# A hybrid decoder step: cached latents turned as raw float32 rows and split behind the turn, pacing constant 7.1 to 6.7

## Chip, cores and metric

The kernel runs on one core of a Trainium2 chip. The metric is the device time of one execution in microseconds (us); the number compared is the median of several executions. PE is the matrix engine, DVE the vector engine, ACT the scalar engine, POOL the GpSimd engine, SP the engine that issues most transfers.

## The reference, cut to what matters

One step of a one-layer decoder over 1024 prompt tokens and 8 sample batches of 8 tokens. One input projection yields all branches; the change lies in the attention of the sample batches over their cached past:

```
ckv_past = cache_ckv[page_table]            # (8 batches, 2048 keys, 256 features)
kpe_past = cache_kpe[page_table]            # (8, 2048, 32)
q_abs  = einsum('bthd,rhd->bthr', q_nope, w_uk)
s_past = einsum('bthr,bpr->bhtp', q_abs, ckv_past) + einsum('bthd,bpd->bhtp', q_pe, kpe_past)
...
p = softmax(concat([s_past, s_new]) * ATTN_SCALE)
o_lat = einsum('bhtp,bpr->bthr', p_past, ckv_past) + einsum('bhts,bsr->bthr', p_new, c_kv)
```

Beside it, and independent of it, stands the big product h @ W_in for all 1088 tokens.

## The kernel before, in words

Products with float32 accuracy are made of float32r passes: a number is split into `hi` (rounded to float32r, on ACT or POOL) and `lo` (the rest, on DVE), and `mm3` (lines 76 to 81) issues three passes hi·hi, hi·lo, lo·hi. Where accuracy asks for no product, as in a transpose (`tp`, line 67), one pass is enough.

The attention of the sample goes through blocks: 8 batches, each with four blocks of 512 cached keys (j = 0 to 3; 32 such blocks in all) and one small block of its own new tokens (j = 4). A block of 512 keys goes through these steps.

- `fetch` (line 623): POOL issues an indirect gather of 512 KB into `raw` (two buffers). POOL rounds it to the hi half of `nat`, DVE takes the lo half (lines 645, 646); `nat` too has two buffers. Rotary keys go through `skn` in the same way.
- `turn_keys` (line 651): PE turns rows into columns: two transposes of the rotary keys (`ptk`) and sixteen of the latents (`ptt`, four for each of hi and lo and of two feature halves), each 128 by 128. Four of them fill a PSUM bank, and each bank is copied out to a tile `tt`, hi banks by ACT and lo banks by DVE (line 669).
- `attend` (line 673): scores (`pss`: four passes of 512 columns, one for each `tt`, and two short ones), maximum and exponential on ACT and DVE (`stmp`, `spr`), transposes of the probabilities (`ptp`), their split (`spt`), and the weighted sum of the latents in their natural layout (`spo`: eight passes over `nat`). After the fifth block of a batch the parts are put together (`sacc`) and turned (`pto`).

Between these steps PE is given dense work: `dense` yields the remaining input projection in triples of passes of 362 or 364 columns (`pj`). How much stands between two steps is decided by a counter, `clk`, that adds an estimate for each pass issued (`cost`, line 60: 4.18e-4 us for each column, whatever the kind of pass). `sample_attention` (line 742) turns the next block when the counter is `PACE` beyond the end of the turn before. The order is then laid out, engine by engine, by a list scheduler that may move a row a little; each engine runs its rows strictly in that order. When the sample's attention is done, what is left of the dense work follows without gaps, then the q latents, the latents of the prompt, its attention, and the output.

Of the kernel before, what the change touches and what calls it, by code (L numbers as in the profile page):

```python
# [9 lines left out]
F32 = mybir.dt.float32  # L10
# [8 lines left out]
P = 128  # L19
D = 1024  # L20
NP = 1024            # prompt tokens
NB, NT = 8, 8        # sample batches, tokens each
# [9 lines left out]
NU = 3 + NP + NB * 11            # convolution input with its histories  # L32
# [3 lines left out]
# columns of the per-feature vectors  # L36
V_BSH, V_BSC, V_NW, V_QW, V_CW, V_CB, V_BA, V_BX, V_LAM, V_H0, V_ST = 0, 8, 16, 24, 26, 42, 46, 50, 54, 58, 90
V_ALL = V_ST + 4 * 24
# columns of the shape constants
# [4 lines left out]
def trunk_step(ctx: ExitStack, tc: tile.TileContext, a, o):  # L44
# [3 lines left out]
    PACE = 7.1  # L48
# [4 lines left out]
    def split(hi, lo, src):  # L53
        """src = hi + lo, each of them in float32r"""
        S.copy(hi, src)  # L55
        V.tensor_tensor(lo, src, f(hi), OP.subtract)  # L56

    clk = [0.0]                 # about how many us of products have been issued
# [12 lines left out]
    def mm4(out, lhs, rhs, start, stop, beside=1):  # L71
        """plain float32 product; beside: how many run at once in other columns of the array"""
        clk[0] += 4 * cost(out) / beside
        T.matmul(out, lhs, rhs, start=start, stop=stop)

    def mm3(out, lhs, rhs, start, stop):
        """float32 product out of three float32r passes; lhs, rhs = (hi, lo)"""
        clk[0] += 3 * cost(out)
        T.matmul(out, lhs[0], rhs[0], start=start, stop=False)  # L79
        T.matmul(out, lhs[0], rhs[1], start=False, stop=False)  # L80
        T.matmul(out, lhs[1], rhs[0], start=False, stop=stop)  # L81
# [7 lines left out]
    g_dram = dram.tile([20, P, N], F32, name="g_dram")      # gA, mA, mB before their sigmoids  # L89

    # ------------------------------------------------------------- constants
    vec = const.tile([P, V_ALL], F32, name="vec")
    cst = const.tile([P, C_ALL], F32, name="cst")
    sgs = const.tile([P, D], F32, name="sgs")            # gate in partial sums; row 9: its bias
# [17 lines left out]
    ats = const.tile([P, 4, NS], F32, name="ats")        # attention of the sample, feature by token  # L112

    def rms_pow(out, ss, width, tmp):
        """out = (ss / width + eps) ** -0.5"""
        n = out.shape[0]
        G.tensor_scalar(tmp, ss, 1.0 / width, EPS, OP.mult, OP.add)  # L117
        G.tensor_tensor(out, tmp, nhalf[:n], OP.pow)

    # features of the recurrent branch: convolution input, then gated output  # L120
    # (the first two tiles hold weights before)
# [3 lines left out]
    # ================================================== everything that is projected from h  # L125
    with ExitStack() as px_:
# [3 lines left out]
        sc = hp.tile([P, KC, 32], F32, name="sc")        # silu(c)  # L130
        hs = hp.tile([P, KC, NS], F32, name="hs")        # h of the sample
# [5 lines left out]
        def weights(src, halves=(0, 1), w=None):  # L137
            """one tile of 128 columns: [p, k, 128] as hi, lo"""
# [16 lines left out]
        # -------------------------------------------- h, feature by feature  # L155
        with ExitStack() as pb, tc.manual_schedule(engines={mybir.EngineType.PE}):
# [4 lines left out]
            # silu(c)  # L161
            S.activation(sc, cT, AF.Sigmoid)
            V.tensor_tensor(sc, sc, cT, OP.mult)
            # softplus(-lambda), with log1p(e) = 2 atanh(e / (2 + e))
# [20 lines left out]
            # shift and scale of every feature: [feature, prompt | 8 batches]  # L185
# [8 lines left out]
            def ada_sum(aw):  # L194
                """rows 32 t + j: partial sums over k of c_j @ 256 columns"""
# [29 lines left out]
            def x_norm(i):  # L225
                """128 tokens over their rms"""
# [9 lines left out]
            def x_turn(i):  # L236
                """feature by token"""
# [8 lines left out]
            def h_part(k, s, n):  # L246
                """modulated features of some tokens; two tiles of the recurrent branch serve until that needs them"""
# [64 lines left out]
        # -------------------------------------------- the other projections  # L312
# [6 lines left out]
        def project(w, done, groups=GRP, beside=()):  # L319
            """128 columns of the input projection; beside: what is issued after each group of tokens"""  # L320
# [10 lines left out]
        def gate_sums(k, q):  # L331
            """partial sums of 128 columns of the modulation's gate: rows 32 t + j"""
# [21 lines left out]
        def gate_lru(c):  # L354
            """the recurrent branch times silu(gB)"""
            def done(g, s, n, ps):
                U = L[c]
                sg = cc.tile([P, 364], F32, name="ev", bufs=2)
                # silu(g) = g / 2 (1 + tanh(g / 2)); tanh has its place beside exp
# [17 lines left out]
        def dense():  # L377
            """the projections that no one waits for, to be put between the steps of what has to wait"""
# [17 lines left out]
        def fill(us):  # L396
            """dense work for about so many us"""
# [4 lines left out]
        with ExitStack() as pd:  # L402
# [11 lines left out]
            # rows of 16 keys (rotary keys) and of 4 keys (latents): (page * 8 + p % 8) * 4 + quarter  # L414
# [3 lines left out]
            cnew = cc.tile([NS, 512], F32R, name="cnew")      # new latents of the sample: hi | lo  # L418
            knew = cc.tile([NS, 64], F32R, name="knew")       # new rotary keys of the sample: hi | lo
            ctn = cc.tile([P, 2, 2, NS], F32R, name="ctn")    # new latents, feature by token: [r, hi | lo, half, token]  # L420
            ktn = cc.tile([P, NS], F32R, name="ktn")
            V.memset(f(ktn[64:128]), 0.0)
            qa = cc.tile([P, 2, H, NS], F32, name="qa")       # queries of the latents: [r, half, head, token]
            qr = cc.tile([P, H, NS], F32, name="qr")          # rotary queries, four times along the rows
            ol = cc.tile([P, 2, H, NS], F32, name="ol")       # attended latents
# [3 lines left out]
            def kv_finish(i, m, ps, tmp_pool, ck_pool):  # L429
                """latent and rotary key of up to 128 tokens, and their outputs"""  # L430
# [10 lines left out]
                for j in range(2):                      # the other half beside  # L441
# [8 lines left out]
            # ---------------------------------------- queries and new keys of the sample, token by token  # L450
            def sample_queries(kq):
                ps = bank("pkvq")               # [kv; q]
# [22 lines left out]
                # normed q latent  # L475
# [21 lines left out]
                # queries: [half of the heads and token, head, 64 | rotary | rotary swapped]  # L497
# [14 lines left out]
                # feature by [half of the heads, head, token]  # L512
# [9 lines left out]
                # through the keys' up projection  # L522
# [7 lines left out]
            # ---------------------------------------- convolution, gates and scan of the recurrent branch  # L530
            def recurrence(p2):
                for c in range(4):
# [37 lines left out]
                    # 1 - exp(2 log_a) = tanh(-log_a) (1 + a a)  # L570
# [4 lines left out]
                    # the position before each sample starts its recurrence: a = 0, b = h0  # L575
# [9 lines left out]
            def interleave(*streams):  # L585
                """streams yield how long their next step has to wait; meanwhile the others, else dense work"""
# [19 lines left out]
            # ---------------------------------------- attention of the sample  # L606
            with ExitStack() as pq:
# [15 lines left out]
                def fetch(b, j):  # L623
                    """page rows as hi and lo"""
                    if j == 0:
                        # [r, half, hi | lo of (head, token)], and the rotary part for even and odd keys
# [22 lines left out]
                    return nat, kn  # L649

                def turn_keys(b, j, got):
                    """keys by rows: feature by token"""
# [3 lines left out]
                    nat, kn = got  # L656
# [5 lines left out]
                    tt = [[None, None], [None, None]]  # L662
                    for i in range(2):
                        for r in range(2):
                            pt_ = bank("ptt", F32R, (P, 4, P))
                            for k in range(4):
                                tp(pt_[:, k, :], nat[:, i, KEY[k], P * r:P * r + P], ident_r)
                            t_ = p4.tile([P, 512], F32R, name="tt", bufs=6)
                            (S.copy if i == 0 else V.tensor_copy)(t_, f(pt_).rearrange("p a b -> p (a b)"))  # L669
                            tt[r][i] = t_  # L670
                    return tt, kt_

                def attend(b, j, got, turned):
                    """512 keys of the past, or the new ones (j = 4): their part of the attention, with its own maximum"""
# [4 lines left out]
                    # scores: products, then the sum of the hi and lo halves of the queries and the maximum  # L679
# [12 lines left out]
                    else:                       # the keys of other batches have no part  # L692
# [10 lines left out]
                    # probabilities by keys, and the latents that they weigh  # L703
# [8 lines left out]
                    for k in range(nt):  # L712
                        for i in range(2):
                            mv = got[0][:, i, KEY[k], :] if j < 4 else cnew[:, 256 * i:256 * i + 256]
# [8 lines left out]
                    # the parts together  # L723
# [18 lines left out]
                def sample_attention():  # L742
                    todo = [(b, j) for b in range(NB) for j in range(5)]
                    got = fetch(*todo[0])
                    live = []                   # [ready, stream]
# [36 lines left out]
            # values out of the latents, two heads at a time  # L782
# [24 lines left out]
        # -------------------------------------------- latents of the prompt, and the first keys and queries  # L807
# [5 lines left out]
        # keys of a head, feature by token: 64 latent rows, then the rotary key twice  # L813
# [42 lines left out]
        def latent_turn(i, acc):  # L856
            """latents of 128 tokens, feature by token"""
# [7 lines left out]
        def rotary_keys(g, acc):  # L865
            """rotary keys of half of the prompt, feature by token"""
# [6 lines left out]
        with ExitStack() as pq:  # L873
            # q latent without its 1 / rms: that goes into the rotary tables. Its squares stay where tables
            # and keys come later
# [28 lines left out]
            # rotary keys of the prompt, twice side by side  # L904
# [481 lines left out]
```

## Time and profile before

| what | value |
|---|---|
| median of 3 runs | 1009.61 us (1009.12 to 1012.59) |
| span of the profiled execution | 1014.5 us |
| PE busy | 979.5 us, 97% of the span |
| DVE, ACT, POOL busy | 653.5, 505.5, 235.8 us (64%, 50%, 23%) |
| sample attention, first to last transpose of latents | 197.8 to 554.5 us |

The profiled execution's own time is its span; no other part of it is shown. It lies 4.9 us over the median of the runs shown. A busy share counts a pipelined pass longer than the time by which it delays the next one, so prices of passes are best read from the distance between starts or from the chain of work that ended last, where pieces do not overlap.

### The profile page before, as it was taken

To read this page: it belongs to the slowest core of one execution; us is meant where nothing else is said; L and a number is where in the kernel's file an instruction comes from. 1 tells how busy PE (TensorE), PEld (TensorE's weight loads), DVE (VectorE), ACT (ScalarE), POOL (GpSimd) and SP (SyncE) were. 2 spreads that over 40 slices of the span, in tenths; PEclk is the share of its full clock that TensorE was granted. 3 is DMA by queue.
4 is the path that set the end of the run, shared out by engine and by line. 5 is a ranking of instruction groups with operands and counts; after the bars stand their busy time and mean duration, and the time that the engine had idled before them with its cause. 6 is when DMAs were issued, how large, how long until landed. Compare 5 with 4: busy or idle time off the path is not lost.

```text
span 1014.5 us, 17199 instructions
## 1 busy us (share of the span) xinstructions
PE 979.5 (97%) x6317; PEld 885.0 (87%) x6317; DVE 653.5 (64%) x1486; ACT 505.5 (50%) x1182; POOL 235.8 (23%) x312
## 2 busy tenths in 40 slices
PE   4899999999999999999999999999999999999997
PEld 3676999899999999999999889888888899998886
DVE  5773664556565767665565536888879976882643
ACT  6455655444444444444444433767768854651211
POOL 5442221321112111111110013534444400000101
PEclk9998999999999999999999999999999999999999
DMA  9852123444333332243222212100010155652331
GB/s 327 297 136 78 55 95 103 139 139 137 106 114 105 102 104 87 86 123 112 85 93 67 75 52 62 38 13 21 12 32 11 36 179 167 197 176 72 127 102 63
DMA packets 52102, 104.67 MB, mean 103 GB/s; under 512 B 8177, under 2 KB 23601, under 8 KB 50994
## 3 DMA queue, kind: packets, MB, share of 16 engines
q1 hardware_dynamic: 46626, 84.69, 25.9%
q0 software_dynamic: 5392, 18.88, 6.5%
q8 instruction: 50, 0.82, 0.3%
q14 instruction: 34, 0.28, 0.1%
HBM read 85.58 MB, written 16.92 MB: 101 GB/s over the span
## 4 chain that ended last, share of the span: by engine, by line
PE 72%; DVE 4%; ACT 3%; issue 1%; DMA 0%; POOL 0%; POOLq 0%; SPq 0%; DVEq 0%; ACTq 0%
PE pj L79 9%; PE pj L81 8%; PE pj L80 8%; PE ptt L69 4%; PE pss L65 4%; PE spo L65 3%; PE py L79 3%; PE py L80 3%; PE py L81 3%; PE pout L81 3%; PE pout L80 3%; PE pout L79 3%; PE ptr L1019 2%; PE po L1036 1%; PE ptp L69 1%; PE sc L79 1%
## 5 line engine op out<-in xcount | busy, mean ns | idle before, releaser
L79 PE MATMUL pj<-hh,whi 128*128 128x362 f32 (+2 forms) x656 | 228.4, 348 | 0.0
L80 PE MATMUL pj<-hl,whi 128*128 128x362 f32 (+2 forms) x656 | 219.0, 334 | 0.0
L81 PE MATMUL pj<-hh,wlo 128*128 128x362 f32 (+2 forms) x656 | 218.9, 334 | 0.0
L79 PEld LDWEIGHTS pj<-hh,whi 128*128 128x128 f32 x656 | 124.5, 190 | 10.4 <-issue 4.9
L80 PEld LDWEIGHTS pj<-hl,whi 128*128 128x128 f32 x656 | 124.8, 190 | 2.3 <-issue 0.9
L81 PEld LDWEIGHTS pj<-hh,wlo 128*128 128x128 f32 x656 | 124.6, 190 | 2.2 <-issue 0.9
L645 POOL TENSOR_SCALAR nat<-raw 128x1024 fp32r<-128x1024 f32 x32 | 34.5, 1078 | 192.4 <-PE spo L65 189.0
L1005 POOL TENSOR_SCALAR pr<-pr,mx 128x128 f32<-128x128 f32 (+3 forms) x64 | 49.4, 772 | 88.5 <-DVE mx L1004 80.1
L1002 ACT ACTIVATE pr<-sc,mx 128x128 f32<-128x128 f32 (+3 forms) x64 | 47.7, 746 | 13.5 <-DVE mx L1000 12.5
L1000 DVE TENSOR_REDUCE mx<-sc 128x1 f32<-128x128 f32 (+3 forms) x64 | 48.1, 751 | 7.6 <-PE sc L998 7.3
L69 PE MATMUL ptt<-ident_r,nat 128*128 128x128 f32 x512 | 49.8, 252 | 1.1 <-POOL nat L645 1.1
L56 DVE TENSOR_TENSOR spt<-ptp,spt 128x256 fp32r<-128x256 f32 (+1 forms) x40 | 15.2, 380 | 51.3 <-ACT spt L55 51.2
L69 PEld LDWEIGHTS ptt<-ident_r,nat 128*128 128x128 f32 x512 | 46.3, 142 | 1.4 <-POOL nat L645 1.4
L56 DVE TENSOR_TENSOR ptl<-ptr,pth 128x512 fp32r<-128x512 f32 (+1 forms) x80 | 45.4, 576 | 3.3 <-ACT pth L55 2.3
L1260 ACT ACTIVATE ot<-xo 128x512 f32<-128x512 f32 (+2 forms) x19 | 11.5, 606 | 72.2 <-DVE xo L1259 67.9
L1019 PE MATMUL ptr<-ident,pr 128*128 128x128 f32 x288 | 45.2, 275 | 1.5 <-DVE ptl L56 1.3
L689 ACT COPY stmp<-pss 64x512 f32<-64x512 f32 (+1 forms) x40 | 20.0, 500 | 52.7 <-PE pss L65 52.5
L117 POOL TENSOR_SCALAR ost<-ost 128x1 f32<-128x1 f32 (+1 forms) x9 | 2.9, 325 | 183.7 <-DVE ost L1263 183.7
L55 ACT CAST pth<-ptr 128x512 fp32r<-128x512 f32 (+1 forms) x80 | 40.0, 502 | 10.2 <-PE ptr L1019 9.2
L56 DVE TENSOR_TENSOR wlo<-wraw,whi 128x512 fp32r<-128x512 f32 x58 | 39.9, 703 | 6.5 <-ACT whi L55 6.3
L646 DVE TENSOR_TENSOR nat<-raw,nat 128x1024 fp32r<-128x1024 f32 x32 | 39.1, 1222 | 7.3 <-POOL nat L645 7.1
L669 DVE CAST tt<-ptt 128x512 fp32r<-128x512 f32 x64 | 41.1, 682 | 3.6 <-PE ptt L69 1.0
(469 smaller groups left out, 2629.5 us busy)
## 6 DMA issues: line engine op xcount, KB each, us to landing
wraw<-w_in SPq DMA_DIRECT2D x60, 256.0 KB, 3.3
sg<-g_dram SPq DMA_DIRECT2D x16, 544.0 KB, 3.8
aw<-ada_ss SPq DMA_DIRECT2D x8, 1024.0 KB, 7.6
g_dram<-ev SPq DMA_DIRECT2D x40, 181.0 KB, 3.0
wraw<-ada_g SPq DMA_DIRECT2D x16, 256.0 KB, 2.9
oraw<-w_out SPq DMA_DIRECT2D x16, 256.0 KB, 3.6
xo<-xp SPq DMA_DIRECT2D x8, 512.0 KB, 5.2
out_y<-xo SPq DMA_DIRECT2D x16, 256.0 KB, 2.1
```

What stands on the lines that cost most here:

```text
L55: S.copy(hi, src)
L56: V.tensor_tensor(lo, src, f(hi), OP.subtract)
L65: T.matmul(out, lhs, rhs, start=start, stop=stop)
L69: T.transpose(out, x, eye)
L79: T.matmul(out, lhs[0], rhs[0], start=start, stop=False)
L80: T.matmul(out, lhs[0], rhs[1], start=False, stop=False)
L81: T.matmul(out, lhs[1], rhs[0], start=False, stop=stop)
L669: (S.copy if i == 0 else V.tensor_copy)(t_, f(pt_).rearrange("p a b -> p (a b)"))
L1000: V.tensor_reduce(mx[:, 1:2], ps[:, :nch, :used], AX.XY, OP.max, negate=True)
L1002: S.activation(pr[:, :w].rearrange("p (a b) -> p a b", a=nch), ps[:, :nch, :used], AF.Exp, bias=mx[:, 1:2], accum_out=mx[:, 2:3])
L1005: G.tensor_scalar(pr[:, :w], pr[:, :w], mx[:, 3:4], 0.0, OP.mult, OP.add)
L1019: T.transpose(ps[:, k, i, :], pr[i][:, kc * P:(kc + 1) * P], ident)
```

## The change

`turn_keys` no longer turns the hi and lo halves of `nat`. It turns the gathered rows `raw` themselves as plain float32, four transposes for each of the two feature halves (eight in place of sixteen), and splits each bank when it is copied out of PSUM: ACT writes the hi tile, then DVE subtracts it from the bank and writes the lo tile. `nat` is still made as before, for `spo` alone. The counter's estimate for a turn falls with the eight transposes, and `PACE` falls from 7.1 to 6.7. Comment lines and docstrings that the change also drops are left out here.

```diff
-    PACE = 7.1
+    PACE = 6.7
...
-                    return nat, kn
+                    return raw, nat, kn
...
-                    nat, kn = got
+                    raw, nat, kn = got
...
-                    tt = [[None, None], [None, None]]
-                    for i in range(2):
-                        for r in range(2):
-                            pt_ = bank("ptt", F32R, (P, 4, P))
-                            for k in range(4):
-                                tp(pt_[:, k, :], nat[:, i, KEY[k], P * r:P * r + P], ident_r)
-                            t_ = p4.tile([P, 512], F32R, name="tt", bufs=6)
-                            (S.copy if i == 0 else V.tensor_copy)(t_, f(pt_).rearrange("p a b -> p (a b)"))
-                            tt[r][i] = t_
+                    tt = []
+                    for r in range(2):
+                        pt_ = bank("ptt", F32, (P, 4, P))
+                        for k in range(4):
+                            tp(pt_[:, k, :], raw[:, KEY[k], P * r:P * r + P], ident)
+                        t_ = [p4.tile([P, 512], F32R, name="tt", bufs=6) for _ in range(2)]
+                        split(*t_, pt_.rearrange("p a b -> p (a b)"))
+                        tt.append(t_)
                     return tt, kt_
...
-                            mv = got[0][:, i, KEY[k], :] if j < 4 else cnew[:, 256 * i:256 * i + 256]
+                            mv = got[1][:, i, KEY[k], :] if j < 4 else cnew[:, 256 * i:256 * i + 256]
```

Over the whole program the rows of PE fall by 256 (512 transposes `ptt` before, 256 now); on DVE 64 copies of `tt` become 64 subtractions of the same size; on ACT, POOL and SP no row is added or removed.

PE, at the third block of the second batch (j = 2), before: the probabilities of the block ahead are turned, a dense triple, then the turn.

```order
L69 MATMUL ptp<-ident,spr 128x64 x4
L79 MATMUL pj<-hh_104,whi 128x364
L80 MATMUL pj<-hl_112,whi 128x364
L81 MATMUL pj<-hh_104,wlo 128x364
L69 MATMUL ptk<-ident_r,skn 128x128 x2
L69 MATMUL ptt<-ident_r,nat 128x128 x16
```

PE at the same turn with the change: eight transposes that read `raw`, then the probabilities of the block ahead.

```order
L69 MATMUL ptk<-ident_r,skn 128x128 x2
L69 MATMUL ptt<-ident,raw 128x128 x8
L69 MATMUL ptp<-ident,spr 128x64 x4
L79 MATMUL pj<-hh_107,whi 128x362
L80 MATMUL pj<-hl_115,whi 128x362
L81 MATMUL pj<-hh_107,wlo 128x362
```

The transposes halve and no longer stand behind `nat`; the rows around them move by a triple or two, and no dense row is lost.

DVE, at the first block of the second batch (j = 0), before: the lo half of `nat` stands ahead of the two copies of `tt`.

```order
L719 TENSOR_TENSOR soj<-spo,so_2624 64x256
L734 SCALAR_TENSOR_TENSOR sacc<-soj,sst,sacc 64x256
L646 TENSOR_TENSOR nat<-raw,nat 128x1024
L669 CAST tt<-ptt 128x512 x2
L56 TENSOR_TENSOR spt<-ptp,spt 64x64
L734 SCALAR_TENSOR_TENSOR sacc<-soj,sst,sacc 64x256
```

DVE at the same place with the change.

```order
L719 TENSOR_TENSOR soj<-spo,so_2575 64x256
L56 TENSOR_TENSOR skn<-kr,skn 128x4x32
L646 TENSOR_TENSOR nat<-raw,nat 128x1024
L56 TENSOR_TENSOR tt<-ptt,tt 128x512
L56 TENSOR_TENSOR spt<-ptp,spt 64x64
L350 COPY ev<-pj 128x362
L56 TENSOR_TENSOR tt<-ptt,tt 128x512
L734 SCALAR_TENSOR_TENSOR sacc<-soj,sst,sacc 64x256
```

The two lo tiles stand apart now, the second behind a copy of a projection, and both still behind the lo half of the next `nat`.

POOL, in the second batch (buffer numbers tell the blocks apart: 2523, 2602, 2735, 2837 are j = 0 to 3), with the change: what a gather waits for.

```order
L645 TENSOR_SCALAR nat_2525<-raw_2523 128x1024 [waits DMASW0_49,PE_49]
L645 TENSOR_SCALAR nat_2604<-raw_2602 128x1024 [waits DMASW1_49,PE_49]
L642 DMA raw_2735<-cache_ckv,idx_807 128x1024 [waits DVE_49,PE_49]
L635 DMA kr_3556<-cache_kpe,idx_807 128x512 [waits DMASW4_49,DVE_49]
L642 DMA raw_2837<-cache_ckv,idx_807 128x1024 [waits PE_49,Pool_49]
L645 TENSOR_SCALAR nat_2737<-raw_2735 128x1024 [waits DMASW2_49,PE_49]
```

Before, a gather waited for DVE alone (the lo half of `nat` two blocks back); now it also waits for PE, which turns that `raw`.

## Rows read from the trace of the kernel before

**Rows 1.** The page: its span, and the busy time of PE.
```profile
span 1014.5 us, 17199 instructions
PE 979.5 (97%) x6317; PEld 885.0 (87%) x6317; DVE 653.5 (64%) x1486; ACT 505.5 (50%) x1182; POOL 235.8 (23%) x312
```

**Rows 2.** Busy time by engine over the sample's attention; PEclk is the granted clock.
```profile
187.90:571.20 383.30, 381.65 (x2671) 356.39 (x2669) 229.69 (x578) 165.11 (x423) 74.76 (x74) 1.00 0.34 104
```

**Rows 3.** Waits of PE in 187 to 571 us: total, times, longest.
```profile
PE ptt L69 <- POOL nat L645: 1.1, 1, 1.1
PE ptk L69 <- DVE skn L56: 0.6, 1, 0.6
```

**Rows 4.** Chain that ended last, from one turn to the next: start, duration, what.
```profile
358.17 1.37 PE ptt L69 x16
359.54 0.23 PE pj L79
...
361.56 0.17 PE pj L79
...
362.06 1.15 PE pss L65 x6
...
368.42 1.37 PE ptt L69 x16
```

**Rows 5.** Tile ptt: count, duration in ns (min/median/max), first and last start.
```profile
L69 PE MATMUL ptt<-ident_r,nat x512: 244/251/328, 197.8 to 554.5; 128*128 128x128 f32 x171
L669 ACT CAST tt<-ptt x64: 586/594/607, 198.3 to 554.4; 128x512 fp32r<-128x512 f32 x64
L669 DVE CAST tt<-ptt x64: 669/680/693, 201.0 to 555.0; 128x512 fp32r<-128x512 f32 x64
```

**Rows 6.** Chain that ended last, prompt attention: float32 transposes of probabilities.
```profile
712.04 0.44 PE ptr L1019 x4
712.48 0.12 PE po L1036
```

**Rows 7.** Timeline of PE in the prompt attention; a row ends later than the next starts.
```profile
700.81 0.63 PE L1019 MATMUL ptr<-ident,pr 128*128 128x128 f32 x4
...
701.40 0.28 PE L1037 MATMUL po<-ptl,v 128*128 128x256 f32 x1
```

**Rows 8.** Tile ptr: its copy to hi and its subtraction, as the change needs them.
```profile
L55 ACT CAST pth<-ptr x80: 362/582/609, 640.9 to 811.7; 128x512 fp32r<-128x512 f32 x48, 128x256 fp32r<-128x256 f32 x32
L56 DVE TENSOR_TENSOR ptl<-ptr,pth x80: 404/673/693, 642.4 to 812.6; 128x512 fp32r<-128x512 f32 x48, 128x256 fp32r<-128x256 f32 x32
```

**Rows 9.** Tile raw: POOL's hi half of nat, and the gather from issue to landing.
```profile
L645 POOL TENSOR_SCALAR nat<-raw x32: 1047/1054/1419, 196.7 to 546.6; 128x1024 fp32r<-128x1024 f32 x32
...
DMA to landing us min/median/max: 4.3/4.8/6.6
```

**Rows 10.** Windows around the first turn and the end of the sample's attention, as rows 2.
```profile
195.00:204.00 9.00, 7.36 (x43) 6.52 (x42) 6.07 (x10) 3.95 (x10) 5.36 (x4) 0.81 0.50 166
577.00:585.00 8.00, 7.50 (x38) 6.17 (x37) 4.10 (x9) 6.10 (x18) 0.00 (x0) 0.79 0.41 119
```

**Rows 11.** Chain that ended last: a plain float32 product of 512 columns (two records).
```profile
610.32 0.86 PE qss L914 x2
```

**Rows 12.** Timeline of DVE in a first block of a batch.
```profile
387.31 0.47 DVE L734 SCALAR_TENSOR_TENSOR sacc<-soj,sst,sacc 64x256 f32<-64x256 f32 x1
...
389.40 0.68 DVE L697 CUSTOM_DVE_ANT_0 spr<-pss,stmp 64x512 f32<-64x512 f32 x1 [1.41 <-ACT stmp L689]
...
398.56 1.23 DVE L646 TENSOR_TENSOR nat<-raw,nat 128x1024 fp32r<-128x1024 f32 x1 [0.19 <-POOL nat L645]
399.70 0.53 DVE L361 SCALAR_TENSOR_TENSOR ev<-ev,pj 128x364 f32<-128x364 f32 x1
```

**Rows 13.** Timeline of ACT in the same block.
```profile
388.78 0.58 ACT L689 COPY stmp<-pss 64x512 f32<-64x512 f32 x1 [3.21 <-PE pss L65]
...
391.18 0.72 ACT L700 ACTIVATE spr<-spr,sst 64x512 f32<-64x512 f32 x1
```

## The prediction

> **What bounds the kernel now.** I read the page first. PE is busy for 979.5 of 1014.5 us, no other engine for more than two thirds [rows 1]. A busy share proves nothing by itself, so I looked at the stage of the change next, by the windows view: from 187.9 to 571.2 us PE is busy for 381.65 of 383.3 us at a granted clock of 1.00 (the level of 2.4 GHz) while DVE works 60% of it, ACT 43% and POOL 20% [rows 2]. The list of waits then says that in this stage PE stood still for another engine twice, 1.7 us in all, both at the very first turn [rows 3]. The stage is PE's own queue from end to end, and what is taken out of that queue comes off the time, as long as no wait fills the hole. The dense triples are a fixed amount: what the blocks do not use is run after them, so a shift between the two is neither gain nor loss. The 32 turns are a part of that queue, 512 transposes with starts from 197.8 to 554.5 us [rows 5].
>
> **The sixteen transposes that go.** Their mean duration of some 250 ns [rows 5] is not their price, since passes overlap. The chain of work that ended last has no overlap: there a turn takes 1.37 us, and the triple behind it starts with a pass of 0.23 us where a triple deep inside dense work has 0.17 [rows 4]. Together 1.43 us for each block.
>
> **The eight that come.** A plain float32 transpose of 128 by 128 with `ident` is done 288 times in the prompt attention, so its price is on the trace. On the chain four of them take 0.44 us, exit included, with a pass behind them that costs its usual 0.12 [rows 6]; twice that is 0.88 us. The timeline gives a second reading: four start at 700.81, the second pass behind them at 701.40, 0.59 us later, of which one pass of 0.12 [rows 6] is not theirs, so 0.47, twice 0.95 [rows 7]. The saving for each block lies between 1.43 - 0.95 = 0.48 and 1.43 - 0.88 = 0.55 us. I take 0.52, the middle, because both are readings of the same kind of row. Times 32 blocks: **-16.6 us**, bounds -15.4 and -17.6.
>
> Here a rule stands against the row. The Trainium skill, "FP8 and Floating Point Precision", section "TensorE Precision Notes", has true float32 go through the array in four passes. By that rule eight float32 transposes would be more work than sixteen in float32r, and the sum would lose its gain. Rows 6 and 7 show that a transpose is not charged so: 0.11 us each, beside 0.086 (1.37 / 16) for one in float32r. What remains of the rule is the third rival.
>
> **DVE and ACT.** The copies change kind, not size. The hi copy from PSUM took 594 ns and takes about 582 in the prompt attention; the lo tile took 680 ns as a copy and about 673 as a subtraction [rows 5, 8]. So both engines keep their load: 0 us. But the order gets longer: before, two hi banks went to ACT and two lo banks to DVE side by side; now each subtraction waits for ACT.
>
> Where does that chain run late? In most blocks it doesn't: from the start of the eight transposes both banks are full after 0.9 us, the hi tiles follow on ACT at 0.58 each, and the last subtraction ends about 2.6 us after the start (0.5 for the first bank, 0.6, twice 0.68, hand-overs of about 0.1). In the kinds of block that I followed through the new order the last score pass is due at 3.5 us or later. The exception is the first block of a batch, 8 of 32. There DVE's row order puts the lo half of the next `nat` ahead of the first subtraction, and a copy of a projection between the two. That `nat` waits for the weighted sum that ends just before the turn. Sum from there: POOL's hi half 1.05 [rows 9], DVE's lo half 1.23 [rows 12], then 0.67, 0.53 for the copy [rows 12], 0.67 [rows 8], 4.15 us, and with an estimate of 0.4 for four hand-overs 4.6. PE reaches the fourth score pass after 0.13 + 0.9 (turn), about 2.0 (four triples of three passes at 0.17 [rows 4]), three score passes (0.23 each, the 1.15 of the six less the short pair [rows 4]), the two-pass sum over new tokens (two passes of 0.12 [rows 6]) and one triple of 0.5: 4.5 us. No slack. The softmax behind it is tight as well: copy 0.58, reduction 0.68, a `sacc` row of 0.47 in between, exponential 0.72 [rows 12, 13], 2.45 us and hand-overs of some 0.6, against six triples (3.0 us) that cover it. I put a wait of 0.3 us on each of the 8, **+2.4 us**, bounds 0 (the queue is early) and 8 (1 us each). What queues behind is PE itself, so this is paid in full.
>
> **`nat` and the gathers.** `nat` is now needed only for the weighted sum, nearly a block later, so its 1.05 and 1.23 us are covered by more dense work than before. A gather into `raw` now waits until PE has turned the block two back. It lands 4.3 to 6.6 us after issue [rows 9] and is needed two turns later, which before was two times 10.2 us (358.17 to 368.42 [rows 4]) and now is some 9.3 each; the cover is over 10 us. POOL waits in its queue for that turn with `nat` rows behind it, and these are due later still. 0 us; if the cover were gone, 5 us at a block. PACE: dense triples between two turns fall from about 11 to 10, the triples left over (about 42) run after the attention, two thirds of them behind the last product `puv`. 0 us.
>
> **The two ends.** The first turn waits 1.1 us for `nat` [rows 3]; with the change it needs only the gathered rows: **-1.1 us**, bounds 0 (the gather itself was late) and -2.1, since behind this hole the clock is granted at half for some microseconds (0.81 over nine [rows 10]) and that may go too. At the end `puv` waits for weights (PE idle for 0.5 of eight us), and the clock falls again (0.79 over these eight [rows 10]). The weights' loads still start when the last block frees its buffers, and about as much PE work lies between: 0 us, bounds -1.9 and +2.
>
> **Sum.** -16.6 + 2.4 - 1.1 = -15.3 us. The profiled span of 1014.5 would become 999.2. Its 4.9 us over the median is the profiled execution's own and is carried over: 1009.6 - 15.3 = **994.3 us**.
>
> **Rivals.**
> 1. Forecast, 0.80: PE's queue gets shorter by what the rows say. Own range: -15.4 - 0 + 8 + 2 = -5.4 at worst and -17.6 - 2.1 - 1.9 = -21.6 at best; 988 to 1004.
> 2. The serial copy chain becomes the wait, 0.09. For it speaks that DVE is behind POOL, ACT and itself in the tight blocks, against it the idle 40% of DVE. It would have to reach all 32 blocks: at 0.3 us each and 1 us in the eight, 7 + 8 = 15 of the 17.7 us go back and the time is about 1007. From 0.5 us in each of the 32 on, it takes all.
> 3. Float32 transposes cost more in this place than in the prompt attention, 0.04: the slower side. The nearest row of real float32 work is a product of 512 columns, 0.86 us [rows 11], a quarter of which is 0.215 for 128 columns; eight are 1.72, 0.29 over the 1.43 of now, times 32 is +9: about 1018. The point from which it decides is 1.43 / 8 = 0.18 us for one. Against it speak 288 rows of the same shape.
> 4. The turns were not on the path, and what they free is only moved, 0.07: dense work, thinned around the blocks, comes after them and waits there for weights or banks. Then the time stays at 1006 to 1010. Against it: PE hardly waits in this stage, and weights are loaded a tile (12 us of dense work) ahead.
>
> **How the numbers follow.** Predicted is the likeliest, 994.3. The range takes in its bounds, cut at the top where the costs of the eight blocks would all have to be near their worst: 988.5 to 1001.5. Half a percent is 5 us, about what a measurement of this kernel can tell from no change: faster is below 1004.6. Case 1 gives it in full, case 2 in about half; case 4 and the rest of 2 are no change, case 3 is slower, and I add little for mechanisms not seen: faster 0.86, same 0.09, slower 0.05.
>
> **What the profile after would show.** 256 transposes `ptt` with starts 0.11 us apart, a turn of 0.88 us on the chain; the last one near 535 us instead of 554; PE busy all through the stage; the wait for `nat` at the first turn gone. Wrong would be: waits of PE for DVE at `pss` or for ACT at `ptp` of more than 0.5 us in more than the first blocks of batches; starts of `ptt` 0.2 us apart; a granted clock below 1.00 inside the stage; or PE idle among the dense triples after the attention.

## The result and the profile after

The changed kernel takes 992.35 us (median of 4 runs, 990.65 to 995.75) beside 1009.94 us of the kernel before (4 runs): ratio 0.9825, 95% interval 0.9802 to 0.9848. The profiled execution spans 989.5 us where before it was 1014.5 [rows 1]. These 25.0 us are more than the 17.6 between the medians, since the profile of before lay over its median; the first experiment below takes that apart. A span is some 2 us shorter than the time of the same execution (989.5 beside 991.34 us here).

The page of the changed kernel: its span, and the busy time of each engine.

```profile
span 989.5 us, 16762 instructions
PE 957.2 (97%) x6061; PEld 863.3 (87%) x6061; DVE 652.6 (66%) x1486; ACT 503.0 (51%) x1182; POOL 240.8 (24%) x312
```

Busy time by engine over the sample's attention and the dense work behind it, then over the first turn; columns as in [rows 2].

```profile
187.00:575.00 388.00, 385.99 (x2523) 355.40 (x2522) 238.56 (x586) 176.85 (x454) 78.57 (x72) 1.00 0.35 109
191.00:195.00 4.00, 3.44 (x23) 3.19 (x24) 2.42 (x6) 2.53 (x8) 1.36 (x2) 1.00 0.74 281
```

PE is busy for 386.0 of 388.0 us at a granted clock of 1.00, as before [rows 2], and the low clock of the first turn [rows 10] is gone.

The waits of PE from 185 to 620 us: total, times, longest.

```profile
PE ptp L69 <- ACT spr L700: 1.4, 2, 0.7
PE pkv L80 <- DVE kvl L56: 0.6, 1, 0.6
PE ptt L69 <- DMA raw<-cache_ckv,idx: 0.5, 1, 0.5
```

The wait for `nat` [rows 3] is gone; 0.5 us for the gather itself stands in its place, and there are two new waits of 0.7 us at `ptp`.

The tile `ptt`: count, duration in ns (min/median/max), first and last start.

```profile
L69 PE MATMUL ptt<-ident,raw x256: 272/273/327, 191.9 to 512.8; 128*128 128x128 f32 x128
L55 ACT CAST tt<-ptt x64: 576/590/599, 192.6 to 513.1; 128x512 fp32r<-128x512 f32 x64
L56 DVE TENSOR_TENSOR tt<-ptt,tt x64: 670/681/692, 194.2 to 513.9; 128x512 fp32r<-128x512 f32 x64
```

The copies kept their price (590 and 681 ns for 594 and 680 [rows 5]). One turn on the timeline of PE, with a dense pass behind it. The chain that ended last is followed back only to 983.86 us in this profile, so a turn is read here from start to start.

```profile
242.67 1.06 PE L69 MATMUL ptt<-ident,raw 128*128 128x128 f32 x8
243.49 0.41 PE L79 MATMUL pj<-hh,whi 128*128 128x362 f32 x1
243.74 0.33 PE L80 MATMUL pj<-hl,whi 128*128 128x362 f32 x1
```

Eight transposes take 0.82 us (242.67 to 243.49) and the pass behind them 0.25, where before it was 1.37 and 0.23 [rows 4]; within a turn the starts are 0.109 us apart.

The whole stage, from the first `ptk` to the end of the last dense pass, can be split without rest by the starts on PE's timeline. Dense passes are counted at 0.173 us, their mean behind one another, and there are 1401 in each column. A turn is taken from its second `ptk` to the second row behind its last `ptt`, less the usual price of that row.

| us | before, first profile | before again (below) | change | new turn, pace 7.1 (below) |
|---|---|---|---|---|
| head: first `ptk` to first `pss` | 6.4 | 6.3 | 3.8 | 3.5 |
| 31 further turns | 47.4 | 47.4 | 32.1 | 31.0 |
| other rows of the blocks, waits included | 99.0 | 99.0 | 99.3 | 99.5 |
| dense passes among the blocks | 224.9 (1300) | 224.9 (1300) | 209.2 (1209) | 224.9 (1300) |
| behind the last `pto` | 25.8 (89 dense) | 24.2 (89) | 39.0 (180) | 23.4 (89) |
| of that, beyond the dense passes | 10.4 | 8.9 | 7.8 | 8.0 |
| stage | 403.4 | 401.8 | 383.3 | 382.2 |

### The profile page after: what moved, and what is told of

The parts are those of the page before. It is cut to its first block, busy times and chain, and to the rows that moved or that the text cites. A ratio compares the mean times of both kernels' runs of the same rounds, so it can differ in the third digit from the quotient of the medians.

```text
span 989.5 us, 16762 instructions
## 1 busy us (share of the span) xinstructions
PE 957.2 (97%) x6061; PEld 863.3 (87%) x6061; DVE 652.6 (66%) x1486; ACT 503.0 (51%) x1182; POOL 240.8 (24%) x312
## 5 line engine op out<-in xcount | busy, mean ns | idle before, releaser
L79 PE MATMUL pj<-hh,whi 128*128 128x362 f32 (+2 forms) x656 | 224.3, 342 | 0.0
L642 POOL DMA_INDIRECT raw<-cache_ckv,idx x32 | 36.9, 1152 | 96.7 <-DVE skn L56 70.5
L56 DVE TENSOR_TENSOR tt<-ptt,tt 128x512 fp32r<-128x512 f32 x64 | 41.6, 683 | 8.4 <-ACT tt L55 8.3
L55 ACT CAST whi<-wraw 128x512 fp32r<-128x512 f32 x58 | 34.1, 621 | 18.5 <-PE pj L80 18.5
L717 ACT COPY so<-spo 64x256 f32<-64x256 f32 x40 | 14.8, 369 | 51.4 <-PE spo L65 51.3
L1036 PE MATMUL po<-pth,v 128*128 128x256 f32 x128 | 37.5, 317 | 1.4 <-DVE v L56 1.4
```

The lines of the kernel that those rows point to most:

```text
L642: nc.gpsimd.indirect_dma_start(raw.rearrange("p k r -> p (k r)"), None, ckv_rows, bass.IndirectOffsetOnAxis(ap=idx[:, j, b:b + 1], axis=0))
L1036: T.matmul(po[:, :256], st, mv[0], start=k == 0, stop=False)
```

## The experiments

**The kernel before, profiled again.** Nothing is edited.

> The kernel before, unchanged, for a second profile. Its first profile spans 1014.5 us, some 5 us over the median of its runs. Two theories on what the profile after lacks besides the transposes. Theory A (the kernel's own): the queue at the first turn (wait 1.1 us, then half clock until 201.8) and at puv (PE idle, then half clock until 584) stand in every execution; then this profile shows both again, the stage from the first ptk to the last pj takes 402 to 404 us, and only the ends differ (the 2.1 us wait for the weights of pkvq gone, span 1008 to 1010). Theory B (the execution's): one or both are late transfers of that one execution; then the stage takes 398 to 401 us here.

Measured: 1011.1 us, ratio 1.0008 (0.9997 to 1.0018); span 1008.7. The first window is the first turn, the second what follows it, the third `puv`; then PE's waits.

```profile
191.00:195.00 4.00, 2.28 (x14) 1.91 (x14) 2.01 (x4) 2.08 (x7) 2.14 (x2) 0.82 0.76 291
195.00:200.00 5.00, 5.00 (x29) 4.75 (x29) 4.07 (x6) 2.19 (x5) 3.57 (x3) 0.80 0.28 52
573.00:581.00 8.00, 7.47 (x44) 6.44 (x43) 3.58 (x9) 5.13 (x16) 0.00 (x0) 1.00 0.33 93
```

```profile
PE ptt L69 <- POOL nat L645: 1.1, 1, 1.1
PE pkvq L74 <- DMA kqr<-w_kvq: 0.9, 1, 0.9
```

The wait of the first turn and the half clock behind it (the level of 1.2 GHz: dense passes start 0.30 us apart there, 0.17 at 2.4) stand in both profiles, as theory A has it; that the wait doesn't always bring the half clock, the run of the pace alone shows below. The half clock behind `puv` [rows 10] was that one execution's (theory B): PE idles there for 0.5 us again, at a clock of 1.00. The stage takes 401.8 us, between the ranges of the two theories. Against this profile the change saves 19.2 us of span, 18.5 of them in the stage and 0.6 ahead of it; behind it both take the same. Of the other 5.8 us in 1014.5, 4.2 lie ahead of the first `ptk` (it starts at 195.9 there and at 191.7 here; the wait at `pkvq` was 2.1 us there) and 1.6 in the stage.

**The turn without the pace.**

```diff
-    PACE = 6.7
+    PACE = 7.1
```

> The new turn with the old pace of 7.1. If the gain is the shorter queue of PE (my forecast), 991 to 994 us, within 1.5 us of the change as a whole, and the two waits of ptp for ACT (0.7 us each) shrink, since more dense work stands in between. If the closer pacing is part of the gain (rival), the time lies above 996.

Measured: 989.92 us, ratio 0.9799 (0.9779 to 0.9819), span 988.0. Of the two waits at `ptp` one is left.

```profile
PE ptp L69 <- ACT spr L700: 0.3, 1, 0.3
```

The gain is the turn's. The time lies 1.1 us below the forecast and 2.4 below that of the change; the last pair of runs takes that up. The last turn stands at 530.5 us here and at 512.8 with a pace of 6.7, yet the times hardly differ: dense work moves behind the attention and costs the same there.

**The pace without the turn.**

```diff
-    PACE = 7.1
+    PACE = 6.7
```

> The old turn with the new pace of 6.7. If PE's queue sets the time, what the blocks do not use is run after them and the time stays at 1008 to 1012 us, with the last turn some 12 us earlier. If the pacing is a gain of its own (rival), 1005 or less; if the tighter blocks of the old turn wait, 1013 or more.

Measured, on the kernel before: 1009.12 us, ratio 0.9990 (0.9978 to 1.0002), span 1007.6; the last turn at 530.7 instead of 550.1 us. No effect that can be told from none, though the last turn is 19.4 us earlier where some 12 were expected. PE's waits in the stage, and the clock over the nine us of the first turn:

```profile
PE pss L65 <- DVE tt L669: 1.2, 1, 1.2
PE ptt L69 <- POOL nat L645: 1.1, 1, 1.1
```

```profile
190.00:199.00 9.00, 6.28 (x41) 4.92 (x40) 5.55 (x10) 3.93 (x10) 5.00 (x4) 1.00 0.45 141
```

The wait for `nat` is the same here as in the two profiles of before, and the half clock did not follow it. PE's first turn in this run, then in the second profile of before:

```profile
190.67 0.37 PE L69 MATMUL ptk<-ident_r,skn 128*128 128x128 f32 x2 [0.44 <-DVE skn L56]
...
197.34 1.09 PE L65 MATMUL pss<-tt,qab 128*128 128x512 f32 x3 [1.22 <-DVE tt L669]
198.28 0.40 PE L65 MATMUL pss<-skt,qp 128*128 128x256 f32 x2
```

```profile
191.74 0.36 PE L69 MATMUL ptk<-ident_r,skn 128*128 128x128 f32 x2 [0.67 <-DVE skn L56]
...
198.95 0.40 PE L65 MATMUL pss<-skt,qp 128*128 128x256 f32 x2
```

From the first `ptk` to the short score passes it is 7.6 us at the full clock and 7.2 with the half clock. The rows of PE up to there are the same. At the full clock it gets to the scores earlier and then stands 1.2 us for DVE's `tt`: in this place the half clock cost nothing.

**Every transpose of latents twice.**

```diff
                             tp(pt_[:, k, :], raw[:, KEY[k], P * r:P * r + P], ident)
+                            tp(pt_[:, k, :], raw[:, KEY[k], P * r:P * r + P], ident)
```

> The change with each of the eight transposes of a turn issued twice into the same place: 256 more float32 transposes and nothing else. If a transpose is paid in full in PE's queue at 0.11 us (forecast), +28 to +30 us over the change, about 1021. If the turn were partly hidden (rival 4), less than +15, under 1007. If a float32 transpose were worth a quarter of a 512-column float32 product, 0.215 us (rival 3), +55, about 1047.

Measured: 1020.34 us, ratio 1.0096 (1.0076 to 1.0117). That is 28.0 us over the change, and 28.0 / 256 = 0.109 us for each further transpose; over the change's second measurement below (990.65) it is 29.7, or 0.116. One turn on PE's timeline:

```profile
248.58 1.94 PE L69 MATMUL ptt<-ident,raw 128*128 128x128 f32 x16
250.27 0.41 PE L79 MATMUL pj<-hh,whi 128*128 128x362 f32 x1
```

It takes 1.69 us to the next start where the change has 0.82, again 0.109 for each of the eight. PE pays a float32 transpose in full, and it pays about 0.11, not 0.215: rivals 3 and 4 fall.

**The subtraction made a plain copy.** The lo tile holds the whole value, not the rest.

```diff
-                        split(*t_, pt_.rearrange("p a b -> p (a b)"))
+                        S.copy(t_[0], pt_.rearrange("p a b -> p (a b)"))
+                        V.tensor_copy(t_[1], pt_.rearrange("p a b -> p (a b)"))
```

> The change, but the lo tile is a plain copy of the bank that does not wait for ACT's hi tile (so lo holds the whole value, and the scores are not the reference's). This takes away the serial chain ACT then DVE and leaves both engines their load. If the chain costs only in some tight blocks (forecast), the time falls by 0 to 3 us, to 989 to 992. If the chain is a wait in most blocks (rival 2), it falls by 7 to 15 us, below 985.

Measured: 990.9 us, ratio 0.9813 (0.9792 to 0.9833); stage 383.1 us beside 383.3. But the edit did not take the wait away: each of the 64 copies still starts 0.03 us or more after ACT's copy of its bank has ended. Both read the same bank; that this is the reason is likely, but not shown. What DVE waits for at `tt`, in the change and here, then PE's wait at `ptp` here:

```profile
DVE tt L56 <- ACT tt L55: 8.3, 23, 3.6
```

```profile
DVE tt L670 <- ACT tt L669: 8.3, 23, 3.6
```

```profile
PE ptp L69 <- ACT spr L701: 1.4, 2, 0.7
```

So this run does not test the serial chain; it shows that a copy in place of a subtraction changes nothing. Rival 2 falls by the profile of the change itself. PE waits there for no `tt`, and outside the first blocks of batches the second subtraction ends 2.6 us after the first transpose of its turn, the fourth score pass starting at 4.0 us or later. A first block of the change, on PE and on DVE:

```profile
316.37 0.28 PE L69 MATMUL ptk<-ident_r,skn 128*128 128x128 f32 x2
...
321.42 0.39 PE L65 MATMUL pss<-tt,qab 128*128 128x512 f32 x1
```

```profile
320.08 0.67 DVE L56 TENSOR_TENSOR tt<-ptt,tt 128x512 fp32r<-128x512 f32 x1
```

The second subtraction ends at 320.75, 0.7 us before the fourth score pass. In the very first block it is less than 0.1 us.

**The cheaper kind of transpose.** The eight read the hi half of `nat`; the lo halves of the latents are zero in the scores.

```diff
-                        pt_ = bank("ptt", F32, (P, 4, P))
+                        pt_ = bank("ptt", F32R, (P, 4, P))
...
-                            tp(pt_[:, k, :], raw[:, KEY[k], P * r:P * r + P], ident)
+                            tp(pt_[:, k, :], nat[:, 0, KEY[k], P * r:P * r + P], ident_r)
```

> The change, but the eight transposes read the hi half of nat in float32r in place of raw in float32 (the lo halves of the latents are then zero in the scores). Same number of rows, the cheaper kind, and the old dependence on nat. If only PE's queue counts: 256 transposes at 0.087 in place of 0.109 us are -5.6 us, the first turn's wait for nat comes back (+1 to +2), so 988 to 989 us. If turning raw earlier than nat is ready was a gain in the blocks too (rival), PE waits for POOL's nat and the time is 993 or more.

Measured: 987.0 us, ratio 0.9773 (0.9752 to 0.9793), 1 us below the forecast; stage 379.8 us. From start to start the 256 transposes take 23.3 instead of 28.8 us (-5.5), and the head 5.4 instead of 3.8 (+1.6): the wait for `nat` is back, with the half clock behind it (0.81 from 190 to 199 us). No other wait for `nat` came.

```profile
PE ptp L69 <- ACT spr L700: 1.4, 2, 0.7
PE ptt L69 <- POOL nat L645: 1.1, 1, 1.1
```

**The head of the kernel before, three us later.**

```diff
-                fill(12.0)
+                fill(15.0)
```

> The kernel before with 3 us more dense work ahead of the first turn (12 to 15), so that nat is ready when it comes. This prices the head alone. If the wait and the half clock behind it are what the change takes from the head (forecast -1.1, at most -2.1), the time falls by 1 to 2 us to 1008, the wait at ptt is gone and the stage from the first ptk to the last pj, with the 3 us taken into account, is 1 to 2 us shorter. If the half clock does not come from that wait, it stays and the gain is 1.1 at most.

Measured: 1008.91 us, ratio 0.9997 (0.9981 to 1.0013). The expected 1 to 2 us did not come. The wait at `ptt` is gone, and the next step has taken it over:

```profile
PE pss L65 <- DVE tt L669: 2.0, 1, 2.0
```

The clock stays at 1.00 here. From the first `ptk` to the last `pj` it is 398.1 us with 18 dense passes fewer, 401.2 with these at 0.173: 0.6 us less than 401.8. In the old kernel `nat` was only the first thing that was late.

**A wider pace.** 7.5 in place of 6.7, with the new turn.

> The new turn with a pace of 7.5. With 7.1 the waits inside the blocks were gone and 25 triples were left behind the attention. If waits are all that the pace decides, 989 to 991 us, as with 7.1. If dense work runs out before the last blocks, their steps stand bare and the time is 993 or more.

Measured: 992.25 us, ratio 0.9830 (0.9809 to 0.9851), between the two forecasts. The waits at `ptp` are gone, but only 49 dense passes are left behind `puv`, and then the weights of the next product are late:

```profile
PE pkv L79 <- ACT kvh L55: 1.9, 1, 1.9
```

**The lo half of `nat` on POOL.** The two waits at `ptp` were still open. DVE in the changed kernel around the first of them, then POOL at the same time:

```profile
341.14 0.46 DVE L363 SCALAR_TENSOR_TENSOR L<-ev,L 128x298 f32<-128x298 f32 x1
341.52 1.07 DVE L365 SCALAR_TENSOR_TENSOR L<-ev,L 128x64 f32<-128x64 f32 x1
342.51 0.67 DVE L697 CUSTOM_DVE_ANT_0 spr<-pss,stmp 64x512 f32<-64x512 f32 x1
...
343.12 1.21 DVE L646 TENSOR_TENSOR nat<-raw,nat 128x1024 fp32r<-128x1024 f32 x1
344.26 0.14 DVE L699 TENSOR_SCALAR sst<-sst 64x1 f32<-64x1 f32 x1
```

```profile
341.16 1.35 POOL L645 TENSOR_SCALAR nat<-raw 128x1024 fp32r<-128x1024 f32 x1 [3.52 <-PE spo L65]
```

The exponential needs the small `sst` row, and that stands behind `nat` (1.21 us); before both, L365 took 1.07 us for 64 columns, more than twice what L363 took for 298. I suspected the order first.

```diff
-                    V.tensor_tensor(nat[:, 1], raw, f(nat[:, 0]), OP.subtract)
+                    G.tensor_tensor(nat[:, 1], raw, f(nat[:, 0]), OP.subtract)
```

> The change, with the lo half of nat made by POOL instead of DVE. In the profile of the change PE waits 1.4 us in all, twice at ptp, where DVE has nat's lo half (1.21 us) ahead of the small sst row that the exponential needs. If that row is the cause, these two waits go and the time falls by 1 to 2 us to about 991; the saved 1.2 us of DVE in 32 blocks count for nothing else, as DVE is not the bound. If POOL is slower at it than its slack allows (rival), new waits appear at spo or at ptt for nat and raw, and the time is 994 or more.

Measured: 997.22 us, ratio 0.9875 (0.9853 to 0.9898). Slower than the change, but not by the waits at `spo` or `ptt` that the rival named:

```profile
PE pss L65 <- DVE tt L56: 5.7, 6, 1.0
PE ptp L69 <- ACT spr L700: 0.8, 2, 0.4
```

At `ptp` the two waits shrink to 0.4 us each with L365 still at 1.07, so the place of `nat` in DVE's order is at most a part of them. Six first blocks of a batch wait for DVE. There DVE, then POOL:

```profile
234.41 2.63 DVE L734 SCALAR_TENSOR_TENSOR sacc<-soj,sst,sacc 64x256 f32<-64x256 f32 x1
236.97 1.27 DVE L56 TENSOR_TENSOR tt<-ptt,tt 128x512 fp32r<-128x512 f32 x2
```

```profile
234.33 2.44 POOL L646 TENSOR_TENSOR nat<-raw,nat 128x1024 fp32r<-128x1024 f32 x1
```

A `sacc` row takes 0.47 us [rows 12]. Started while POOL worked on `nat`, it ends about when POOL does. That gave a second theory: DVE is held up by POOL.

**The hi half of `nat` on ACT**, so that POOL only issues gathers in these blocks.

```diff
-                    G.tensor_scalar(nat[:, 0], raw, 1.0, 0.0, OP.mult, OP.add)
+                    S.copy(nat[:, 0], raw)
```

> The change, with the hi half of nat made by ACT instead of POOL, so that POOL reads nothing in the sample's attention. In the profile of the change the DVE row L365 (two inputs in SBUF, 64 columns) takes 0.21 us in two places and 1.07 in two others, where POOL works on nat at the same time, and these two are the places where PE waits 0.7 us at ptp. Theory (DVE is held up by POOL): all four L365 rows take 0.21 us, no sacc row takes over 0.5, the two waits at ptp are gone or below 0.4, and the time is 988.5 to 991. Rival (the late row is a matter of DVE's order alone): L365 becomes short but the waits at ptp stay at 0.7, or ACT's extra 1 us in each block makes new waits, and the time is 991 or more.

Measured: 991.72 us, ratio 0.9809 (0.9791 to 0.9828). The row L365, then PE's waits:

```profile
L365 DVE SCALAR_TENSOR_TENSOR L<-ev,L x4: 218/219/221, 342.9 to 407.2; 128x64 f32<-128x64 f32 x4
```

```profile
PE pss L65 <- ACT tt L55: 1.0, 1, 1.0
PE pss L65 <- DVE tt L56: 0.7, 1, 0.7
```

All four L365 rows take 0.22 us, no `sacc` over 0.48, and the waits at `ptp` are gone with DVE's order unchanged there. The mechanism is shown, and the other profiles bear it out: of the 56 L365 rows in all fourteen, the 12 that run beside a POOL row of `nat` take 1.06 or 1.07 us, the other 44 take 0.21 to 0.23. The time is the same, above what the theory forecast, because at the first turn ACT now has `nat` ahead of `tt`, and that brought 1.7 us of new waits: the second half of the rival.

**The change and the pace of 7.1 side by side.** No further edit.

> The change unchanged, beside the next kernel on the same chip: 991 to 993.5 us. Forecast: 1 to 2.5 us over it, the two waits at ptp being the difference; rival: no difference, and the first comparison was chance.

> The new turn with a pace of 7.1 once more: 989.5 to 991 us if the pace of 7.1 is really the better one, 992 or more if its first runs were chance.

Measured: 990.65 us, ratio 0.9807 (0.9785 to 0.9830), and 990.13 us, ratio 0.9807 (0.9785 to 0.9829). The profiled spans are 989.6 and 987.9 us, like the pair above (989.5 and 988.0), 1.5 to 1.7 apart; the times, 0.5 apart where 1 to 2.5 was forecast, do not tell them apart. No version was found that beats the change measurably and computes the same.

## Why the prediction held

The time lay 2 us below the 994.3 of the forecast. By the steps of the sum, against the second profile of before:

1. **The 32 turns**, forecast -16.6 us (-15.4 to -17.6). The 31 behind the first went from 47.4 to 32.1 us, 0.49 each, -15.8 for 32. With a pace of 7.1 it is 0.53 each. The price held: 0.82 us and 0.08 more for the pass behind, 0.90 where 0.88 to 0.95 was read. At 6.7, 15 of the 32 turns are followed by `ptp`, at 7.1 only 7, and such a turn takes 0.99 us instead of 0.82 to the next start, 0.13 more by the measure of the table, which also counts what the next row pays; eight times that is the 1.1 us between the two paces. The four-pass rule of the Trainium skill ("FP8 and Floating Point Precision", section "TensorE Precision Notes") did not decide here: the doubled turn gives 0.109 us for a float32 transpose beside 0.087 in float32r.
2. **DVE and ACT**, forecast +2.4 us in the first blocks of batches. The size was near, +1.4, and that was luck, for the mechanism was wrong. No first block waited for the subtractions. In the one shown with the plain copies above, the fourth score pass starts 5.05 us after the first `ptk`, where I had summed 4.5, and the second subtraction ends 4.4 us after it, where I had 4.6: 0.7 us of slack where I had found none, mostly because PE takes longer to get there than I had summed. The two real waits lie at `ptp`, in the third blocks (j = 2) of two batches, and come from L365, held up by POOL. One of my own signs of being wrong thus came true, in two blocks: a wait of more than 0.5 us at `ptp` outside the first blocks.
3. **`nat`, gathers and PACE**, forecast 0: confirmed for PACE by the run of the pace alone (0.9990). The marker that I named for it was wrong: the last turn is at 512.8 us and not near 535. I had subtracted the gain and left out that the pace moves 91 more dense passes, 15.7 us, behind the last `pto`; with the old pace it is at 530.5.
4. **The head**, forecast -1.1 us (0 to -2.1). It lost 2.5 us, 0.5 of it the first turn's own saving, so -2.0, inside the bounds but not for the reason that I gave for them. The half clock cost nothing there: in the run of the pace alone the clock stayed at 1.00 and the old head was no shorter, nor did the later start buy more than 0.6 us. Behind the wait for `nat` stood a second one, for DVE's lo half and its copies into `tt` (1.2 and 2.0 us in these two runs). The new turn needs neither half of `nat`, and both waits go at once: from the first `ptk` to the short score passes it is 4.8 us with the change, 7.2 to 7.6 before.
5. **The tail**, forecast 0 (-1.9 to +2): -1.0 against the second profile, the 0.5 us of waits at `puv` and the dearer passes around them. The half clock that I had put into the bounds belonged to one execution.

Together -18.5 us in the stage where -15.3 was forecast; the missing 3.2 are 0.9 of the head, 1.0 of the tail and 2.1 in the blocks (+0.3 instead of +2.4, where the two waits at `ptp` stand against 100 instead of 147 dense passes behind a row of another kind, which are the dearer ones; that these make it up was not tested), less 0.8 of the turns. Carrying the excess of the first profile over was right: against the second, 4.2 of 5.8 us lie ahead of the stage. It was nearer 7 us than 4.9, since a span is some 2 us shorter than the time.

## What to carry to other kernels

Where one engine's queue is full, price a pass by its distance from the next start, on rows of the same kind, and ask what the pass behind it pays; the sum of these was within 1 us of 16. Check a feared serial chain by breaking only its dependence, and see on the trace that it is broken; here it was not. When a wait goes, look for the next one behind it before its length is booked as a gain. Work moved between two engines that are both idle half the time can still cost, if the rows of one stretch under the other.

## What was not expected of the hardware

DVE stands still beside POOL for some rows. With two operands in SBUF, `sacc` took 2.63 us instead of 0.47 while POOL made `nat`, and L365 1.07 instead of 0.21; the subtraction of a bank in PSUM (`tt`) never took more than 0.69, in the four places too where it ran beside POOL's rows of `nat` in that run. The kernel before had it as well: four of its `sacc` rows took 0.93 to 1.29 us. The Trainium skill, "SBUF — State Buffer", section "Who interferes with whom", has this as a rule: a DVE instruction with two SBUF inputs and a GpSimd instruction that reads SBUF exclude each other, and the second to issue waits for the first. The rows agree: POOL's 2.44 us end at 236.77, the `sacc` row that began 0.08 us behind it at 237.04, and POOL's own row was the one that stretched (1.35 instead of 1.05 us) where DVE's L363 had begun first.

A wait of PE is not always followed by a low clock. The 1.1 us at the first `ptt` were in three profiles (both of before, and that with the hi half of `nat`), each at 0.81 over the nine us around; with the same wait in the run of the pace alone the nine us stand at 1.00, and so do those with the 2.0 us at `pss`. What decides it, these runs do not show.
